# A two-layer encoder trunk on one core: the first attention head's K, Q and V of a chunk projected k tile by k tile together

## The chip, the core and the metric

The kernel runs on one core of a Trainium2 chip. Its engines are TensorE (PE, matrix products), VectorE (DVE), ScalarE (ACT) and GpSimd (POOL); SyncE (SP) issues nearly all DMAs. Each engine works through its own queue in order, and the engines wait for one another by semaphores. The metric is the device time of one launch in microseconds (us). The time before is the median of 3 runs.

## The reference, cut to what matters

The input is x with 1024 tokens of 1024 channels, and a conditioning vector c. Two layers follow one another, each a mixer and an MLP, each of these with an RMSNorm that is shifted and scaled by projections of c. Layer 0 mixes by convolution and gating, layer 1 by differential attention with 8 heads. The change touches the place between the MLP of layer 0 and the attention:

```
x = x + gate * (square(relu(hdn @ mlp_w1[0])) @ mlp_w2[0])
shift, scale, gate = split(c_act @ mix_mod_w[1] + mix_mod_b[1], 3)
hdn = modulate(rmsnorm(x, mix_norm_g[1]), shift, scale)
q, k, v = split(hdn @ w_qkv, 3)          # 8 heads, two maps of 64 channels each
p = softmax(q k^T / 8 + bias)            # both maps
attn = p[0] - lam * p[1]                 # then attn @ v, a norm per head, w_out
```

## The kernel before

**Layout.** Channels lie on the 128 partitions, tokens along the free dimension. A k tile is 128 channels (KT = 8 of them), a chunk is 512 tokens (C = 512, NC = 2 of them). x[m][c] is one 128x512 tile.

**Products.** All projections are in float32 accuracy from a rounded format: a weight w is kept as whi (rounded) and wlo (the rest), an activation as hh and hl. mm3 (L132) adds three matmuls into one PSUM tile: whi with hh (L134), whi with hl (L135), wlo with hh (L136). A 128x512 output of 1024 inputs takes 8 k tiles, so 24 matmuls.

**Weights.** prep (L107) loads 128x1024 numbers into raw, casts them to whi on ACT (L112), and makes wlo in one of two ways: with an engine given, that engine subtracts (L114); without, ACT writes the negative of whi (L116) and a DMA from POOL's queue adds the weights to it from memory (L117). raw, whi and wlo have 3 buffers each. A Stream hands out the weights in order and prepares `ahead` more than the one asked for.

**The norm.** Norm.add squares each x tile on ACT (sq, L229) and sums on DVE (ss, L234 and L237). fin sums over the partitions with a matmul against ones (the statistic, L241, two passes), then v on DVE (L202), ln and r on ACT (L211, L213) and three refining steps on DVE (L215 to L217). h then makes for each of the 8 k tiles ht on DVE (L246), hh on ACT (L253) and hl on DVE (L254).

**The end of the MLP.** mlp works in seven products per group, each of 48 matmuls; in the last group, in this order, X3 completes x of chunk 0, Z and X4 complete x of chunk 1 (updates on L746). to_attn(nrm, c), the norm for the attention, is put off by `soon`: a list of functions with a count, which `tick` lowers and calls when it falls below zero. For chunk 0 it is called in the middle of Z. For chunk 1 it is called in the attention, at the second tick there, that is ahead of chunk 0's Q. to_attn also stores x to memory (xsp) for the last head, between the k tiles of h.

**The first head.** qkv(hd) is a generator that projects K, Q and V of one head in units of one output and one chunk. For head 0 the order of the units is K, Q, V of chunk 0, then K, Q, V of chunk 1 (UNITS); for other heads the generator is run between the parts of the softmax of the head before it, as many k tiles as QUOTA says. A unit takes a PSUM bank (tag mm, 2 buffers), 24 matmuls, and its evictions: K by two casts and two subtractions (L913 to L916), Q likewise and with copies by DMA (L920 to L928), V by a copy, four transposes and a split (L931 to L936). The scores S have 2 buffers of two banks each. Head 0 has nothing to run beside: its generator is emptied before the first softmax. ws, the stream of the heads' weights, prepares one ahead; its low halves are made on DVE for head 0 and the first weight of head 1, on POOL from then on.

**What sets the order.** The program is written once, straight through; a planner then decides the order on each engine's queue. It plays the program through with estimated durations, and whenever an engine comes free it takes, of the instructions whose inputs are ready and whose buffers are free in its play, the one with the best rank. The rank is the place in the program; `tc.high_priority(offset=n)` moves what stands in it n places ahead. On the chip the queues then run in the order so fixed, whatever is late.

Of the kernel before, what the change touches and what calls it, by code (L numbers as in the profile page):

```python
# [10 lines left out]
F32 = mybir.dt.float32  # L11
# [7 lines left out]
P = 128  # L19
D = 1024  # L20
T = 1024
KT = D // P
C = 512
NC = T // C
H = 8
# [22 lines left out]
def trunk(ctx: ExitStack, tc: tile.TileContext, t_in, out):  # L48
    nc = tc.nc
    dve, act, pool, pe, sp = nc.vector, nc.scalar, nc.gpsimd, nc.tensor, nc.sync  # L50

    def f32(ap):
        return ap.bitcast(F32)

    def opened(**kw):
        return tc.tile_pool(reuse_waits="tile", **kw)
# [29 lines left out]
    def load(dst, src):  # L86
        sp.dma_start(out=dst, in_=src)
# [3 lines left out]
    def bank():  # L91
        return psb[-1].tile([P, C], F32, name="ps", tag="mm")
# [7 lines left out]
    def tick(n=1):  # L100
        for e in later:
            e[0] -= n
        while later and later[0][0] < 0:
            later.pop(0)[1]()
# [27 lines left out]
    def mm3(ps, wh, wl, ah, al, first, last, resumed=False):  # L132

        pe.matmul(ps, wh, ah, start=first, stop=False, skip_group_check=resumed)  # L134
        pe.matmul(ps, wh, al, start=False, stop=False, skip_group_check=resumed)  # L135
        newest[0] = pe.matmul(ps, wl, ah, start=False, stop=last, skip_group_check=resumed)  # L136

    def kcol(k):
        return slice(k * P, (k + 1) * P)
# [117 lines left out]
    def split(out_h, out_l, src, lo_eng=None):  # L257
        act.copy(out=out_h, in_=src)  # L258
        (lo_eng or dve).tensor_tensor(out=out_l, in0=src, in1=f32(out_h), op=ALU.subtract)  # L259


    def open_x():
        st = ExitStack()
        xp = st.enter_context(opened(name="xp", bufs=1, side="right"))
        return st, [[xp.tile([P, C], F32, name=f"x{m}_{c}") for c in range(NC)] for m in range(KT)]

    xst, x = open_x()
# [83 lines left out]
    with opened(name="mix", bufs=1) as mp, ExitStack() as pst:  # L351
        first_ps = ExitStack()
        psb.append(first_ps.enter_context(opened(name="gps", bufs=8, space=PSUM)))
        nrm = Norm()
# [3 lines left out]
        h = [[None] * NC for _ in range(KT)]  # L358
# [80 lines left out]
        psum = pst.enter_context(opened(name="mixps", bufs=6, space=PSUM))  # L439
# [5 lines left out]
        for j in range(4):  # L445
            js = slice(j * C, (j + 1) * C)
            ps = bank()
# [34 lines left out]
        for c in range(NC):  # L482
            vps = [bank() for _ in range(4)]
            for j in range(4):
                wh, wl = wv.get(4 * c + j)
# [26 lines left out]
        ps = bank()  # L512
# [48 lines left out]
        xst, x = open_x()  # L561
# [5 lines left out]
        nrm = Norm()  # L567
# [72 lines left out]
        h = [[None] * NC for _ in range(KT)]  # L640
# [229 lines left out]
    xsp = dram.tile([KT, NC, P, C], F32, name="xsp")  # L870

    def to_attn(nrm, c):
        nrm.fin(c)
        for m in range(KT):
            h[m][c] = nrm.h(c, m, x[m][c], 2)
            load(xsp[m, c], x[m][c])

    mlp(0, 1, to_attn)


# [5 lines left out]
    psum = atps.enter_context(opened(name="atps", bufs=2, space=PSUM))  # L886
    psb.append(psum)
    if True:
        ws = Stream([t_in["wqkv"][m] for hd in range(H) for m in (8 + hd, hd, 16 + hd)], ahead=1, eng=dve)
        SC = -(64 ** -0.5)  # L890
        QUOTA = [(2, 3, 0, 0), (2, 2, 2, 1)] * 4
        QUOTA_LAST = [(2, 2, 0, 0), (2, 2, 1, 1)] * 3 + [(0, 2, 0, 0), (0, 4, 0, 0)]
# [2 lines left out]
        def qkv(hd):  # L895
            K = [ap.tile([P, T], F32R, name=f"K{j}", tag="K", bufs=4) for j in range(2)]
            Vh = ap.tile([P, KT, P], F32R, name="Vh", tag="V", bufs=4)
            Vl = ap.tile([P, KT, P], F32R, name="Vl", tag="V", bufs=4)
            Q = [None] * NC
            res = (K, Q, Vh, Vl)  # L900
            yield res
            for which, c in UNITS[hd > 0]:
                cs = slice(c * C, (c + 1) * C)
                wh, wl = ws.get(3 * hd + which)
                tick()
                ps = bank()
                for k in range(KT):
                    mm3(ps, wh[:, kcol(k)], wl[:, kcol(k)], h[k][c][0], h[k][c][1], k == 0, k == KT - 1)
                    if k < KT - 1:
                        yield None  # L910
                with tc.high_priority(offset=300):
                    if which == 0:
                        act.copy(out=K[0][0:64, cs], in_=ps[0:64])  # L913
                        act.copy(out=K[1][64:128, cs], in_=ps[64:128])
                        dve.tensor_tensor(out=K[0][64:128, cs], in0=ps[0:64], in1=f32(K[0][0:64, cs]), op=ALU.subtract)
                        dve.tensor_tensor(out=K[1][0:64, cs], in0=ps[64:128], in1=f32(K[1][64:128, cs]), op=ALU.subtract)  # L916
                    elif which == 1:
                        qs = [ap.tile([P, C], F32R, name="Q", tag="Q", bufs=10) for _ in range(4)]
                        Q[c] = qs
                        act.activation(out=qs[0][0:64], in_=ps[0:64], func=AF.Copy, scale=SC)  # L920
                        act.activation(out=qs[2][64:128], in_=ps[64:128], func=AF.Copy, scale=SC)
                        dve.scalar_tensor_tensor(out=qs[1][0:64], in0=ps[0:64], scalar=SC, in1=f32(qs[0][0:64]),
                                                 op0=ALU.mult, op1=ALU.subtract)
                        dve.scalar_tensor_tensor(out=qs[3][64:128], in0=ps[64:128], scalar=SC, in1=f32(qs[2][64:128]),
                                                 op0=ALU.mult, op1=ALU.subtract)
                        for q in (0, 1):
                            load(f32(qs[q][64:128]), f32(qs[q][0:64]))
                            load(f32(qs[2 + q][0:64]), f32(qs[2 + q][64:128]))  # L928
                    else:
                        vT = tmp.tile([P, C], F32, name="vT", tag="ss", bufs=2)  # L930
                        act.copy(out=vT, in_=ps)  # L931
                        pt = bank()
                        for n in range(4):
                            pe.transpose(pt[:, n * P:(n + 1) * P], vT[:, n * P:(n + 1) * P], ident)
                        vs = slice(c * 4, c * 4 + 4)
                        split(Vh[:, vs, :].rearrange("p a b -> p (a b)"), Vl[:, vs, :].rearrange("p a b -> p (a b)"), pt)  # L936
                yield None
# [125 lines left out]

        wo = Stream([t_in["wo1"][m] for m in range(KT)], ahead=0, eng=pool)
        gen = qkv(0)
        cur = next(gen)
        for _ in gen:
            pass
        ws.eng = pool
        tick(9)  # L1070
        xst.close()
        condp.close()
# [42 lines left out]
    xst, x = open_x()  # L1115
# [3 lines left out]
    with opened(name="wops", bufs=8, space=PSUM) as psum:  # L1119
# [8 lines left out]
        h = project(wo.get, o, ks8, 2, 3, part=(mid, (w7h, w7l)))  # L1128
# [88 lines left out]
```

## Time and profile before

| | |
|---|---|
| median of 3 runs | 2280.48 us (2279.56 to 2282.11) |
| the profiled execution | 2281.83 us |
| its span, first to last instruction | 2279.8 us |
| PE busy | 2193.8 us (96%) |
| DVE busy | 1819.4 us (80%) |
| ACT busy | 1214.2 us (53%) |
| POOL busy | 222.3 us (10%) |
| mean granted clock of PE | 0.989 |

Times in the trace are counted from the first instruction. A row of the timeline has the start, the time from the first start to the last end of the instructions merged in it, the engine, the line, the operation, output and inputs, the count, and in brackets how long the engine stood idle before it and what ended that. Matmuls are pipelined and their ends are modelled, so consecutive rows overlap, and the distance between starts is what a matmul costs. The granted clock is the share of full speed that PE was given.

### The profile page before, as it was taken

What the parts mean: (1) busy time and instruction counts of PE and PEld (TensorE: products, weight loads), DVE (VectorE), ACT (ScalarE), POOL (GpSimd) and SP (SyncE); (2) the same over time, 40 slices, a digit from 0 to 9 for tenths busy, and PEclk for the clock granted to TensorE, in tenths of its full rate; (3) what the DMA queues carried; (4) which work ended last, traced back from release to release, by engine and by line L of the source; (5) the groups of instructions that cost most, each with busy time, mean ns of one, the idle gap of its engine ahead of it and who ended that gap; (6) DMA issues with size and microseconds to landing.
All of it is one profiled execution on the core that took longest, in us unless ns stands there. A gap on an engine that the chain in (4) does not pass through costs nothing. (4 is left out here: it accounts for less than half of the span.)

```text
span 2279.8 us, 27567 instructions
## 1 busy us (share of the span) xinstructions
PE 2193.8 (96%) x10144; PEld 1803.2 (79%) x10144; DVE 1819.4 (80%) x2555; ACT 1214.2 (53%) x1790; POOL 222.3 (10%) x138
## 2 busy tenths in 40 slices
PE   4999898999999999989999999999999999999997
PEld 3778676878888888868888888877778888888886
DVE  7899879995976967978887887885799659577597
ACT  5677646633535435446566666653475354353455
POOL 0485000000000000001111110110000000000003
PEclk9999999999999999989999999999999999999999
DMA  9474774658267275343444433452362561633702
GB/s 352 123 158 108 242 229 174 260 181 292 100 218 271 89 254 193 103 151 55 90 105 84 110 74 69 107 166 82 123 231 86 168 212 56 226 125 122 246 39 74
DMA packets 118038, 350.37 MB, mean 154 GB/s; under 512 B 21040, under 2 KB 23984, under 8 KB 116880
## 3 DMA queue, kind: packets, MB, share of 16 engines
q1 hardware_dynamic: 113728, 333.41, 45.0%
q0 software_dynamic: 4176, 15.21, 3.8%
q8 instruction: 80, 1.31, 0.2%
q14 instruction: 54, 0.44, 0.1%
HBM read 294.99 MB, written 53.58 MB: 153 GB/s over the span
## 5 line engine op out<-in xcount | busy, mean ns | idle before, releaser
L135 PE MATMUL ps<-b,whi 128*128 128x512 f32 (+1 forms) x1808 | 701.4, 389 | 5.9 <-DVE b L259 5.9
L134 PE MATMUL ps<-b,whi 128*128 128x512 f32 (+1 forms) x1808 | 692.3, 389 | 6.3 <-ACT b L258 4.9
L136 PE MATMUL ps<-b,wlo 128*128 128x512 f32 (+1 forms) x1808 | 695.0, 389 | 1.6 <-DVE wlo L259 1.6
L258 ACT CAST whi<-raw 128x1024 fp32r<-128x1024 f32 (+1 forms) x225 | 236.5, 1051 | 355.9 <-PE ps L135 318.5
L135 PEld LDWEIGHTS ps<-b,whi 128*128 128x128 f32 x1808 | 340.7, 188 | 80.0 <-DVE b L259 9.7
L134 PEld LDWEIGHTS ps<-b,whi 128*128 128x128 f32 x1808 | 341.1, 189 | 78.7 <-ACT b L258 6.2
L136 PEld LDWEIGHTS ps<-b,wlo 128*128 128x128 f32 x1808 | 341.1, 189 | 72.1 <-DVE wlo L259 2.0
L259 DVE TENSOR_TENSOR wlo<-raw,whi 128x1024 fp32r<-128x1024 f32 (+1 forms) x225 | 274.8, 1221 | 139.5 <-ACT whi L258 137.2
L134 PE MATMUL ps<-hh,whi 128*128 128x512 f32 x576 | 230.8, 403 | 15.0 <-ACT hh L253 12.5
L135 PE MATMUL ps<-hl,whi 128*128 128x512 f32 x576 | 228.9, 399 | 5.6 <-DVE hl L254 5.5
L136 PE MATMUL ps<-hh,wlo 128*128 128x512 f32 x576 | 227.7, 399 | 3.2 <-DMA wlo<-in_wa 3.2
L965 ACT ACTIVATE L<-L,mn 128x1024 f32<-128x1024 f32 x128 | 147.1, 1150 | 90.8 <-DVE mn L963 89.4
L746 DVE SCALAR_TENSOR_TENSOR x<-ps,mod,x 128x512 f32<-128x512 f32 x220 | 160.7, 751 | 41.3 <-PE ps L136 40.7
L963 DVE CUSTOM_DVE_ANT_0 L<-S,B 128x1024 f32<-128x1024 f32 x128 | 156.0, 1223 | 34.8 <-PE pt L985 17.5
L114 POOL TENSOR_TENSOR wlo<-raw,whi 128x1024 fp32r<-128x1024 f32 x24 | 64.3, 2680 | 1058.0 <-PE S L960 684.6
L258 ACT CAST b<-f 128x512 fp32r<-128x512 f32 x192 | 118.1, 619 | 76.8 <-PE ps L136 75.1
L134 PEld LDWEIGHTS ps<-hh,whi 128*128 128x128 f32 x576 | 110.5, 192 | 41.4 <-ACT hh L253 15.5
L259 DVE TENSOR_TENSOR b<-f,b 128x512 fp32r<-128x512 f32 x192 | 129.7, 690 | 10.3 <-ACT b L258 10.3
L135 PEld LDWEIGHTS ps<-hl,whi 128*128 128x128 f32 x576 | 110.4, 192 | 30.5 <-DVE hl L254 8.7
L136 PEld LDWEIGHTS ps<-hh,wlo 128*128 128x128 f32 x576 | 110.7, 192 | 28.6 <-DMA wlo<-in_wa 3.6
L151 DVE CUSTOM_DVE_ANT_0 mraw<-mraw,cact 128x1024 f32<-128x1024 f32 x96 | 116.6, 1222 | 12.6 <-DMA mraw<-in_modw 12.6
L735 ACT COPY f<-ps 128x512 f32<-128x512 f32 x96 | 56.0, 588 | 123.5 <-PE ps L136 123.3
(201 smaller groups left out, 3469.8 us busy)
## 6 DMA issues: line engine op xcount, KB each, us to landing
b<-tspl SPq DMA_DIRECT2D x168, 512.0 KB, 5.2
raw<-in_wm SPq DMA_DIRECT2D x128, 512.0 KB, 4.8
mraw<-in_modw SPq DMA_DIRECT2D x96, 512.0 KB, 4.6
tspl<-b SPq DMA_DIRECT2D x56, 512.0 KB, 5.3
raw<-in_wqkv SPq DMA_DIRECT2D x24, 512.0 KB, 7.2
raw<-in_wo SPq DMA_DIRECT2D x17, 512.0 KB, 5.0
x<-in_xT SPq DMA_DIRECT2D x32, 256.0 KB, 5.5
tsr<-tsp SPq DMA_DIRECT2D x8, 1024.0 KB, 10.0
```

The source lines that it names most:

```text
L114: eng.tensor_tensor(out=lo, in0=raw, in1=f32(hi), op=ALU.subtract)
L134: pe.matmul(ps, wh, ah, start=first, stop=False, skip_group_check=resumed)
L135: pe.matmul(ps, wh, al, start=False, stop=False, skip_group_check=resumed)
L136: newest[0] = pe.matmul(ps, wl, ah, start=False, stop=last, skip_group_check=resumed)
L151: i = dve.tensor_tensor_reduce(out=raw, in0=raw, in1=cact, op0=ALU.mult, op1=ALU.add, scale=1.0, scalar=0.0, accum_out=acc)
L258: act.copy(out=out_h, in_=src)
L259: (lo_eng or dve).tensor_tensor(out=out_l, in0=src, in1=f32(out_h), op=ALU.subtract)
L735: act.copy(out={"X1": c11, "Y1": c22, "X2": c12}[p], in_=ps)
L746: dve.scalar_tensor_tensor(out=x[m][c], in0=ps, scalar=gate(d, m), in1=x[m][c], op0=ALU.mult, op1=ALU.add)
L963: dve.tensor_tensor_reduce(out=L, in0=S, in1=win, op0=ALU.add, op1=ALU.min, scale=1.0, scalar=3e38, accum_out=mn)
L965: act.activation(out=L, in_=L, func=AF.Exp, bias=mn, scale=-1.0, accum_out=s[:, j:j + 1])
```

## The change

- to_attn makes the norm and all eight pairs hh, hl first and stores x afterwards; for chunk 0 norm and pairs are ranked 200 places ahead.
- For head 0, K, Q and V of a chunk are projected together: three PSUM tiles (the two halves of an S buffer and a bank), and per k tile the three products one after the other. The evictions follow for K, Q and V as before.
- The norm of chunk 1 is called (tick(9)) after the products of chunk 0 and before those of chunk 1.
- The three weights of head 0 are prepared with adding DMAs (no engine given), none ahead; after the products of chunk 1 the stream goes over to one ahead and POOL, so the first weight of head 1 too is made on POOL and asked for only then.

```diff
     def to_attn(nrm, c):
-        nrm.fin(c)
+        with tc.high_priority(offset=0 if c else 200):
+            nrm.fin(c)
+            for m in range(KT):
+                h[m][c] = nrm.h(c, m, x[m][c], 2)
         for m in range(KT):
-            h[m][c] = nrm.h(c, m, x[m][c], 2)
             load(xsp[m, c], x[m][c])
...
-        ws = Stream([t_in["wqkv"][m] for hd in range(H) for m in (8 + hd, hd, 16 + hd)], ahead=1, eng=dve)
+        ws = Stream([t_in["wqkv"][m] for hd in range(H) for m in (8 + hd, hd, 16 + hd)], ahead=0)
...
+            together = []
             for which, c in UNITS[hd > 0]:
                 cs = slice(c * C, (c + 1) * C)
-                wh, wl = ws.get(3 * hd + which)
-                tick()
-                ps = bank()
-                for k in range(KT):
-                    mm3(ps, wh[:, kcol(k)], wl[:, kcol(k)], h[k][c][0], h[k][c][1], k == 0, k == KT - 1)
-                    if k < KT - 1:
-                        yield None
+                if hd == 0:
+
+                    if which == 0:
+                        if c == 1:
+                            tick(9)
+                        w3 = [ws.get(i) for i in range(3)]
+                        S = psum.tile([P, T], F32, name="S", tag="S", bufs=2)
+                        together = [S[:, :C], S[:, C:], bank()]
+                        for k in range(KT):
+                            for i in range(3):
+                                mm3(together[i], w3[i][0][:, kcol(k)], w3[i][1][:, kcol(k)], h[k][c][0], h[k][c][1],
+                                    k == 0, k == KT - 1)
+                        if c == 1:
+                            ws.ahead, ws.eng = 1, pool
+                    ps = together[which]
+                else:
...
-        ws.eng = pool
         tick(9)
         xst.close()
```

More of the change, by code (lines that the diff above doesn't have):

```diff
@@ L901, in qkv @@
             yield res
+            together = []
             for which, c in UNITS[hd > 0]:
                 cs = slice(c * C, (c + 1) * C)
-                wh, wl = ws.get(3 * hd + which)
-                tick()
-                ps = bank()
-                for k in range(KT):
-                    mm3(ps, wh[:, kcol(k)], wl[:, kcol(k)], h[k][c][0], h[k][c][1], k == 0, k == KT - 1)
-                    if k < KT - 1:
-                        yield None
+                if hd == 0:
[13 more added lines that the diff above has]
+                else:
+                    wh, wl = ws.get(3 * hd + which)
+                    tick()
+                    ps = bank()
+                    for k in range(KT):
+                        mm3(ps, wh[:, kcol(k)], wl[:, kcol(k)], h[k][c][0], h[k][c][1], k == 0, k == KT - 1)
+                        if k < KT - 1:
+                            yield None
                 with tc.high_priority(offset=300):
```

## The prediction

> **What bounds the kernel now.** I read the page's busy times first, then the stretches around the place of the change, then who made TensorE (PE) wait there, then that stretch engine by engine in order of time.
>
> ```profile
> PE 2193.8 (96%) x10144; PEld 1803.2 (79%) x10144; DVE 1819.4 (80%) x2555; ACT 1214.2 (53%) x1790; POOL 222.3 (10%) x138
> ```
>
> ```profile
> 940.00:974.50 34.50, 34.49 (x150) 27.71 (x148) 31.39 (x47) 16.49 (x24) 0.00 (x0) 1.00 0.42 143
> 974.50:1027.60 53.10, 44.45 (x166) 33.32 (x166) 40.12 (x61) 27.35 (x42) 3.37 (x2) 0.87 0.41 136
> 1027.60:1080.00 52.40, 52.00 (x273) 43.89 (x272) 42.21 (x73) 31.71 (x51) 4.46 (x3) 1.00 0.27 55
> ```
>
> Columns: stretch, length, then busy time and count for each engine, the granted clock, DMA share. PE is the bound. It is busy for all of the 34.5 us before the stretch from 974.50 and for 52.00 of the 52.40 us after it, at full clock; in between it issues only 166 instructions in 53.10 us, at a mean clock of 0.87. The changed code lies in this stretch: the last MLP product ends at its start, the first head's projections fill it. Both neighbours are limited by PE's own work, so what is won or lost here should reach the end of the program unchanged, and nothing outside it has a gap that the change could close.
>
> What PE waited for in it:
>
> ```profile
> PE ps L135 <- DVE hl L254: 4.2, 3, 2.7
> PE ps L134 <- ACT hh L253: 2.1, 1, 2.1
> PE ps L134 <- ACT ln L211: 2.0, 1, 2.0
> ```
>
> ```profile
> 968.20 1.02 PE L241 MATMUL ps<-ss,ones_r 128*128 128x512 f32 x2
> ...
> 970.45 0.39 PE L134 MATMUL ps<-b,whi 128*128 128x512 f32 x1
> ...
> 973.17 0.39 PE L134 MATMUL ps<-b,whi 128*128 128x512 f32 x1
> ...
> 976.74 0.49 PE L134 MATMUL ps<-hh,whi 128*128 128x512 f32 x1 [2.05 <-ACT hh L253]
> 979.90 0.80 PE L135 MATMUL ps<-hl,whi 128*128 128x512 f32 x1 [2.66 <-DVE hl L254]
> ```
>
> From 970.45 to 973.17 run twelve matmuls: 2.72 / 12 = 0.227 us each. The 166 instructions are 6 x 24 = 144 projection matmuls, 12 of the first scores, 8 short transposes and the two passes of one statistic. 156 x 0.227 = 35.4 us; for the ten others I estimate 1.2 us (the two passes of a statistic end 1.02 us after their start, half of it drain, and a transpose has a quarter of the columns). So 36.6 us of work take 53.1 us: **16.5 us are lost**, 4.2 + 2.1 + 2.0 = 8.3 us as waits, the rest mostly as slow clock. That is the whole sum that can be won, 0.7% of the span.
>
> The slow clock, in consecutive slices of 3.41 us (the same columns):
>
> ```profile
> 985.14:988.55 3.41, 3.41 (x8) 2.55 (x9) 3.41 (x6) 1.53 (x3) 0.00 (x0) 0.50 0.00 0
> 988.55:991.96 3.41, 2.78 (x9) 1.35 (x8) 2.75 (x5) 0.51 (x2) 0.00 (x0) 1.00 0.00 0
> 991.96:995.37 3.41, 1.50 (x7) 1.24 (x8) 2.42 (x5) 2.45 (x4) 0.00 (x0) 1.00 0.01 2
> 995.37:998.78 3.41, 3.41 (x10) 2.63 (x9) 3.34 (x6) 1.25 (x2) 0.00 (x0) 0.51 0.00 0
> ```
>
> At 0.50 the first slice issues 8 matmuls, against 3.41 / 0.227 = 15 at full clock: a slow slice costs 7 x 0.227 = 1.6 us. A slice with PE busy 2.78 us is followed by one at full clock, even though that one is busy only 1.50 us itself; this one is followed by a slow one (0.51). So a hole of about 2 us can cost another 1.6 us.
>
> **The change part by part.** What feeds the first projection, on VectorE (DVE) and ScalarE (ACT):
>
> ```profile
> 965.93 1.22 DVE L114 TENSOR_TENSOR wlo<-raw,whi 128x1024 fp32r<-128x1024 f32 x1
> 967.06 0.69 DVE L237 TENSOR_TENSOR ss<-ss,sq 128x512 f32<-128x512 f32 x1
> ...
> 974.05 0.75 DVE L746 SCALAR_TENSOR_TENSOR x<-ps,mod,x 128x512 f32<-128x512 f32 x1
> 974.72 2.07 DVE L246 SCALAR_TENSOR_TENSOR ht<-x,gA,r 128x512 f32<-128x512 f32 x3
> 976.70 0.75 DVE L746 SCALAR_TENSOR_TENSOR x<-ps,mod,x 128x512 f32<-128x512 f32 x1
> 977.36 1.22 DVE L114 TENSOR_TENSOR wlo<-raw,whi 128x1024 fp32r<-128x1024 f32 x1
> 978.50 0.69 DVE L237 TENSOR_TENSOR ss<-ss,sq 128x512 f32<-128x512 f32 x1
> 979.10 2.07 DVE L254 SCALAR_TENSOR_TENSOR hl<-ht,mod,hh 128x512 fp32r<-128x512 f32 x3
> ```
>
> ```profile
> 968.33 1.03 ACT L112 CAST whi<-raw 128x1024 fp32r<-128x1024 f32 x1
> 970.44 0.69 ACT L211 ACTIVATE ln<-ps,eps 128x512 f32<-128x512 f32 x1 [1.09 <-DVE v L202]
> 971.16 0.63 ACT L213 ACTIVATE r<-ln 128x512 f32<-128x512 f32 x1
> 974.50 1.04 ACT L112 CAST whi<-raw 128x1024 fp32r<-128x1024 f32 x1 [2.70 <-PE ps L135]
> 975.45 0.62 ACT L229 ACTIVATE sq<-x 128x512 f32<-128x512 f32 x1
> 975.99 1.93 ACT L253 ACTIVATE hh<-ht,mod 128x512 fp32r<-128x512 f32 x3
> ```
>
> (a) *Start of the first chunk.* The normalised pairs hh, hl come from a chain: sum of squares (ss), statistic at 968.20, ln, r, ht, hh at 975.99, hl at 979.10. PE is free from 974.50 and gets its second matmul at 979.90. With the low halves made by adding DMAs, DVE loses the 128x1024 subtractions of L114: the one at 965.93 stands ahead of the last ss (967.06 - 965.93 = 1.13 us), the one at 977.36 ahead of hl (978.50 - 977.36 = 1.14 us). The one between the chain's steps near 970 lies beside ln and r on ACT and is worth nothing. The higher rank can drop what else was let in: x at 974.05 (0.67), the cast and the square ahead of hh (975.99 - 975.4 where ht is ready, 0.6), x and ss ahead of hl (977.36 - 976.70, 979.10 - 978.50: 1.26). But the planner fills any slot that it sees free, and rank orders only what is ready together; the rank was already ahead of these in program order. I take half of 2.5. hl then starts at 979.10 - 1.13 - 1.14 - 1.25 = 975.6 and PE's first hl matmul at 976.3. Two hh matmuls fit before: loss 976.3 - 974.5 - 0.45 = 1.4 us; bounds 0.6 (all of the 2.5) and 2.6 (none). Of the old clock loss there, a hole of 1.4 lies between the two cases seen (0.6 and 1.9 us): half of 1.6, 0.8 us, bounds 0 and 3.2.
>
> (b) *Through the first chunk.* Three products together take 9 x 0.227 = 2.04 us per k tile; DVE makes a pair in 2 x 0.66 us (three ht take 976.70 - 974.72 = 1.98), and with six ss of 0.60 among eight pairs in 1.77. So PE is the slower and no longer waits for DVE. But the low halves are late. V's weight slot is freed with the last MLP product (cast at 974.50), Q's at 968.33. From cast to low half:
>
> ```profile
> L116 ACT ACTIVATE wlo<-whi x29: 1037/1057/1065, 17.7 to 333.0; 128x1024 fp32r<-128x1024 f32 x29
> ...
>   PE ps L136: 3.2, 1
> ...
> DMA to landing us min/median/max: 5.3/5.9/9.9
> ```
>
> 1.05 (cast) + 1.06 (negated copy, three more of these on ACT) + 5.9 (median landing of an adding DMA, of 29 before 340 us) = 8.0 us: Q at 976.3, V at 982.5, each up to 1 us later if ACT makes an hh first. GpSimd is idle here (POOL 0.00 in the stretch before), so its queue holds back neither DMA. Until 982.5 PE can run K and Q alone, 1.36 us per pair, about the pace of DVE, and takes up V afterwards: the order loses nothing if the plan foresaw the landing. I take 0.5 us, bounds 0 and 3.2, the one wait that such a DMA caused (3.2 us). By the Trainium skill, "DMA: Bandwidth & Descriptors", Anatomy of one DMA, a DMA from this queue takes an estimated 2.0 + 524288 / 436e3 = 3.2 us; the row's 5.9 is not that, and by the page this term would be 0.
>
> The 72 matmuls are 16.3 us; the first chunk ends at 974.5 + 1.4 + 0.8 + 0.5 + 16.3 = 993.5.
>
> (c) *Between the chunks.* This is new. The second chunk's norm is now called after all of the first chunk's products, so its statistic ranks behind 72 matmuls. Its sums are ready near 988 (first ht near 973, then eight pairs 10.6, six ss 3.6 and an x 0.7 on DVE), but PE then has ready products up to 993.5. From statistic to PE's first use of hh took 976.74 - 968.20 = 8.5 us, of which 0.67 + 0.6 were let in; I take 7.4 us, bounds 7.2 and 8.5. Only the statistic, four transposes and two score matmuls can run meanwhile (1.3 us): 6.1 us idle, bounds 5.9 and 7.2, where the old order had 2.0. A hole that long brings one or two slow slices: 2.5 us, bounds 1.6 and 3.2. The first hl comes some 0.3 us (0.2 to 0.5) later than the three hh matmuls cover: an hl takes 0.75 us, they 0.68, and DVE starts it only when hh is there.
>
> By the Trainium skill, "TensorE: Matmul & The Clock Gate", Part 1, the clock is judged in free-running windows of 3413 ns and falls after an idle one; the slices above have just that length and alternate so, but the one at 995.37 is slow after a hole of only 2.0 us, so here less than an idle window is enough. By the page's rule (only holes above some 3 us count) the 0.8 us of (a) would be 0 and the sum 0.8 us lower.
>
> (d) *Between second chunk and next head.* K, Q and V end together, so the weights of the next head, whose slots they hold, are made at the end, and low halves on GpSimd:
>
> ```profile
> 1019.92 2.40 POOL L114 TENSOR_TENSOR wlo<-raw,whi 128x1024 fp32r<-128x1024 f32 x1 [684.65 <-PE S L960]
> ```
>
> Cast 1.05 + 2.40 after K's last high matmul, nine matmuls (2.0 us) before the end: 1.5 us, and up to 2.3 us more if the four evictions of K and Q go first on ACT. PE has the second half of a score, transposes and two high products to fill with: 1.5 us lost, bounds 0.2 and 2.8; before, V's second chunk covered this (0.3 us lost).
>
> (e) *Nothing else.* The stores of x are issued behind the eight pairs; they are read only in the last head. Accumulating in a score buffer costs nothing, as no score can start before K and Q are out of it.
>
> Sum of the losses after: 1.4 + 0.8 + 0.5 + 6.1 + 2.5 + 0.3 + 1.5 = 13.1 us, against 16.5: **3.4 us won**. The profiled execution took 2281.83 us (span 2279.8 and 2.0 around it), 1.35 above the median of the runs, 2280.48; so 2278.4 in its terms and 2277.1 for the median. All low bounds give 0.6 + 0 + 0 + 5.9 + 1.6 + 0.2 + 0.2 = 8.5 (8.0 won); all high ones 2.6 + 3.2 + 3.2 + 7.2 + 3.2 + 0.5 + 2.8 = 22.7 (6.2 lost).
>
> **The rivals.** *The statistic is taken early.* If PE waits for an hl or a low half when the second sums are ready, the plan puts the statistic in that hole, as it set the one at 968.20 amid products. From 988 the chain ends at 995.4, so the hole is 995.4 - 993.5 = 1.9, not 6.1, and a slow slice less: 3.4 + 4.2 + 1.0 = 8.6 won, 2272. Against it: the backlog of V, which the late low half makes longer.
>
> *The low halves stall PE (slower).* PE takes its queue in order. Where the plan put V's third matmul ahead of K and Q of later tiles, and the DMA lands later than planned, all of PE stands. Price: the slowest landing 9.9 - 5.9 = 4.0 and the wait of 3.2 us seen: 7.2 us, so 2277.1 + 7.2 = 2284. It ends above the time before once the stall passes 3.4 us. For it: V's cast cannot start before 974.50. Against it: 28 of 29 such DMAs made PE wait for nothing, though most were asked for earlier.
>
> *The rank and the pairing change nothing.* If gap fillers stay as they are and the first hole moves from the k tiles to the space between the chunks: terms (a) and (c) at their high ends, 1.2 + 2.4 + 1.1 + 0.7 = 5.4 worse, 2282.5. For it: rank did not keep the cast at 974.50 from standing ahead of hh.
>
> **How the numbers follow.** Likeliest, the trade as summed: 0.45, mostly 2273 to 2282. Early statistic 0.28; low-half stall 0.17; nothing gained 0.10. A measurement of this kernel can tell 0.2%, 4.6 us: faster is below 2275.9, slower above 2285.0. Faster: 0.85 of the early case (0.24), 0.38 of the trade (0.17), together 0.41. Slower: 0.5 of the stall (0.09), 0.2 of the last (0.02), 0.07 of the trade (0.03), together 0.14. Same: 0.45. The range takes in the early case and the stall: 2269 to 2285.
>
> **What would show it.** Right: the first hl matmul by 977; no L114 on DVE before 1010; PE's longest hole between the chunks, ended by an hh of the second chunk, with the statistic directly ahead of it; a slow slice behind it; another hole of 1 to 3 us before the next head, ended by a low half from GpSimd. Wrong: the statistic amid the first chunk's products; a wait of PE for wlo by DMA; PE's first hole still above 4 us; or a time outside the stretch that moves.

## The result: slower by 0.24%, and the profile after

Over 15 runs each the changed kernel took 2284.62 us (2279.83 to 2287.02) and the kernel before 2279.26 us (2273.00 to 2282.34): ratio 1.0024, 95% interval 1.0017 to 1.0031, 5.4 us slower. Predicted were 3.4 us won. The profiled execution of the changed kernel took 2285.2 us, span 2283.4.

Busy times, from the page of the changed kernel:

```profile
PE 2190.3 (96%) x10144; PEld 1801.0 (79%) x10144; DVE 1814.3 (79%) x2551; ACT 1216.8 (53%) x1793; POOL 227.7 (10%) x142
```

The three stretches of the prediction (start:end, length, busy and count of PE, PEld, DVE, ACT, POOL, granted clock, DMA):

```profile
940.00:974.50 34.50, 34.29 (x149) 27.37 (x147) 29.23 (x44) 18.46 (x27) 1.75 (x2) 1.00 0.50 157
974.50:1027.60 53.10, 39.48 (x154) 30.29 (x154) 33.16 (x51) 25.40 (x39) 4.48 (x3) 0.90 0.42 126
1027.60:1080.00 52.40, 50.75 (x263) 41.96 (x264) 43.69 (x76) 31.46 (x52) 6.47 (x3) 1.00 0.26 66
```

In the middle one PE issues 154 instructions instead of 166, and in the third, which held no gap before, it is busy 50.75 us instead of 52.00. What PE waited for in the middle one:

```profile
PE S L134 <- ACT hh L253: 9.3, 2, 6.3
PE S L978 <- DVE K L934: 2.3, 1, 2.3
PE ps L953 <- ACT vT L950: 1.2, 1, 1.2
PE ps L136 <- DMA wlo<-in_wqkv: 0.5, 1, 0.5
PE S L135 <- DVE hl L254: 0.3, 1, 0.3
```

Where these waits lie, in PE's timeline:

```profile
973.92 0.39 PE L136 MATMUL ps<-b,wlo 128*128 128x512 f32 x1
977.30 0.50 PE L134 MATMUL S<-hh,whi 128*128 128x512 f32 x1 [3.00 <-ACT hh L253]
...
978.38 0.80 PE L135 MATMUL S<-hl,whi 128*128 128x512 f32 x1 [0.34 <-DVE hl L254]
...
998.09 0.66 PE L953 MATMUL ps<-ident,vT 128*128 128x128 f32 x4 [1.19 <-ACT vT L950]
998.58 1.02 PE L241 MATMUL ps<-ss,ones_r 128*128 128x512 f32 x2
1005.90 0.80 PE L134 MATMUL S<-hh,whi 128*128 128x512 f32 x1 [6.29 <-ACT hh L253]
...
1024.01 0.39 PE L136 MATMUL ps<-hh,wlo 128*128 128x512 f32 x1
1026.69 0.50 PE L978 MATMUL S<-K,Q 128*128 128x512 f32 x1 [2.29 <-DVE K L934]
...
1028.07 0.48 PE L134 MATMUL ps<-hh,whi 128*128 128x512 f32 x1
```

Chunk 0's last product starts at 996.50, so nothing but a statistic and four transposes runs in the 9.2 us to 1005.90. At the end all three outputs are finished together, and 3.8 us pass before the next head's products.

The third stretch shows in DVE's timeline, in the rows that read the scores of head 0 (L963 before, L982 after). First the kernel before: its first, second and 17th score; then the changed kernel:

```profile
1019.92 1.22 DVE L963 CUSTOM_DVE_ANT_0 L<-S,B 128x1024 f32<-128x1024 f32 x1
1026.18 1.23 DVE L963 CUSTOM_DVE_ANT_0 L<-S,B 128x1024 f32<-128x1024 f32 x1 [3.48 <-PE S L960]
...
1080.20 1.23 DVE L963 CUSTOM_DVE_ANT_0 L<-S,B 128x1024 f32<-128x1024 f32 x1 [0.24 <-PE S L960]
```

```profile
1027.46 1.22 DVE L982 CUSTOM_DVE_ANT_0 L<-S,B 128x1024 f32<-128x1024 f32 x1
1034.03 1.23 DVE L982 CUSTOM_DVE_ANT_0 L<-S,B 128x1024 f32<-128x1024 f32 x1 [2.96 <-PE S L979]
...
1084.95 1.23 DVE L982 CUSTOM_DVE_ANT_0 L<-S,B 128x1024 f32<-128x1024 f32 x1 [0.24 <-PE S L979]
```

The last MLP product starts 0.38 us earlier in this execution than in that of before (973.92 against 974.30), so the scores are read 7.9, 8.2 and 5.1 us later. **PE shift** below is the same comparison for PE: each matmul counts 0.227 us per 512 columns, the start is taken at which PE has done equal work in both traces, and the difference at 940 us is taken off. For the changed kernel it is +2.6 us at 1035 and +5.1 at 1200: 2.6 us are lost in the stretch, 2.5 more in head 0's attention.

What PE waited for in the third stretch, in the kernel before and in the changed one:

```profile
PE S L959 <- DVE mn L963: 0.4, 1, 0.4
```

```profile
PE ps L1015 <- ACT AT L258: 1.1, 1, 1.1
PE S L978 <- DVE mn L982: 0.4, 1, 0.4
PE ps L953 <- ACT vT L950: 0.2, 1, 0.2
```

AT is the transposed result of a softmax, which ACT copies for the product with V. This wait, at 1070.59, is new, and it is at the end of the softmax's chain; what remains of the 2.5 us lies in smaller gaps between matmuls.

### The profile page after: what moved, and what is told of

The parts are those of the page before. It is cut to its first block, busy times and chain, and to the rows that moved or that the text cites. A ratio compares the mean times of both kernels' runs of the same rounds, so it can differ in the third digit from the quotient of the medians.

```text
span 2283.4 us, 27568 instructions
## 1 busy us (share of the span) xinstructions
PE 2190.3 (96%) x10144; PEld 1801.0 (79%) x10144; DVE 1814.3 (79%) x2551; ACT 1216.8 (53%) x1793; POOL 227.7 (10%) x142
## 5 line engine op out<-in xcount | busy, mean ns | idle before, releaser
L134 PE MATMUL ps<-hh,whi 128*128 128x512 f32 x544 | 217.3, 402 | 11.4 <-ACT hh L253 11.0
L136 PE MATMUL ps<-hh,wlo 128*128 128x512 f32 x544 | 214.6, 398 | 2.8 <-DMA wlo<-in_wa 2.3
L135 PE MATMUL ps<-hl,whi 128*128 128x512 f32 x544 | 215.5, 398 | 0.8 <-DVE hl L254 0.7
L982 DVE CUSTOM_DVE_ANT_0 L<-S,B 128x1024 f32<-128x1024 f32 x128 | 155.8, 1222 | 31.0 <-PE pt L1004 16.3
L134 PEld LDWEIGHTS ps<-hh,whi 128*128 128x128 f32 x544 | 103.9, 191 | 35.0 <-ACT hh L253 13.0
L136 PEld LDWEIGHTS ps<-hh,wlo 128*128 128x128 f32 x544 | 104.4, 192 | 27.1 <-DMA wlo<-in_wa 2.7
L135 PEld LDWEIGHTS ps<-hl,whi 128*128 128x128 f32 x544 | 104.4, 192 | 22.9 <-DVE hl L254 1.9
L978 PE MATMUL S<-K,Q 128*128 128x512 f32 x256 | 108.9, 426 | 3.0 <-DVE K L934 2.3
```

Source lines behind the costliest of these rows:

```text
L978: pe.matmul(S[:, sl], self.Q[c][2 * j][:, qs], self.K[j][:, sl], start=True, stop=False)
L982: dve.tensor_tensor_reduce(out=L, in0=S, in1=win, op0=ALU.add, op1=ALU.min, scale=1.0, scalar=3e38, accum_out=mn)
```

## The experiments

Each ratio is to the kernel before, run in the same rounds, 11 or 12 runs of the kernel (six of e2); 0.001 is 2.3 us. "Second score" is its shift against the kernel before, in one profiled execution each, as are the PE shifts.

| kernel | ratio, 95% interval | PE shift at 1035 | second score | PE shift at 1200 |
|---|---|---|---|---|
| changed | 1.0024 (1.0017 to 1.0031) | +2.6 | +8.2 | +5.1 |
| e1 | 1.0022 (1.0013 to 1.0031) | -3.5 | +1.8 | +0.2 |
| e2 | 1.0031 (1.0019 to 1.0042) | +6.1 | +11.7 | +8.6 |
| e3 | 1.0026 (1.0017 to 1.0035) | +5.8 | +11.4 | +8.3 |
| e4 | 1.0014 (1.0005 to 1.0023) | +5.2 | +5.2 | +5.1 |
| e6 | 1.0023 (1.0014 to 1.0032) | +0.7 | +5.4 | +3.1 |
| e8 | 1.0006 (0.9998 to 1.0015) | -3.9 | +1.5 | -0.2 |
| e9 | 1.0002 (0.9993 to 1.0011) | -5.6 | +0.3 | -2.8 |
| e10 | 1.0007 (0.9997 to 1.0016) | -1.8 | +3.4 | +0.7 |
| e11 | 0.9977 (0.9968 to 0.9986) | -5.8 | -5.4 | -4.4 |
| e12 | 1.0024 (1.0016 to 1.0033) | +0.8 | 0.0 | +6.1 |
| e14 | 0.9994 (0.9982 to 1.0005) | -2.1 | -1.7 | -0.7 |
| e15 | 1.0010 (1.0000 to 1.0021) | +0.4 | +0.8 | +1.7 |

**e1, the norm of chunk 1 ahead of chunk 0's products**

```diff
-                        if c == 1:
+                        if c == 0:
                             tick(9)
```

> The changed kernel with one thing undone: the norm of chunk 1 is called ahead of chunk 0's products instead of behind them. The changed kernel stands 5.4 us above the one before (2284.6 against 2279.3).
> Theory A (late statistic: the 9.2 us between chunk 0's last matmul at 996.50 and the next real product at 1005.90 are what the change lost): the sums of chunk 1 are ready at about 989.2 (last ss at 988.61), so the statistic comes near 989 to 990 amid chunk 0's products, and with the 7.3 us from statistic to hh that the changed kernel shows, the first hh of chunk 1 is there at about 996.5, where chunk 0 ends. The hole shrinks from 9.2 to 1 to 2.5 us and one slow slice (1.6 us) goes: 7 to 9 us less in the stretch, 2276 to 2278, 1 to 3 us under the kernel before.
> Rival (the second loss is elsewhere: K, Q and V of chunk 1 end together, so the first softmax begins late and PE waits in head 0's attention at 1062 to 1074 for some 2.5 us whenever chunk 1 ends): the 2.5 us stay or grow, as PE gets to head 1's products earlier too: 2278 to 2280, level with the kernel before.
> Rival (DVE's order: squares and sums of chunk 1 now compete with the pairs of chunk 0 and DVE is the slower one there): PE waits for hl during chunk 0 for as long as is saved behind it: 2282 to 2285.

2284.96 us: at first sight nothing. The trace says otherwise. The statistic runs at 990.83 amid chunk 0's products, PE is 3.5 us ahead of the kernel before at 1035, level with it from 1070 to 1580, and then loses over 7 us in one place:

```profile
1589.17 1.13 PE L1028 MATMUL ps<-sq,ones_r 128*128 128x512 f32 x2 [1.12 <-ACT sq L1026]
1594.80 0.80 PE L134 MATMUL ps<-th,whi 128*128 128x512 f32 x1 [4.50 <-DVE v L1032]
```

The output projection's product waits for the PSUM bank of the head's norm statistic. In the changed kernel this product has the other bank, and no such wait. e8 tests this.

**e8, the same with the other bank**

```diff
-                        if c == 1:
-                            tick(9)
                         w3 = [ws.get(i) for i in range(3)]
                         S = psum.tile([P, T], F32, name="S", tag="S", bufs=2)
                         together = [S[:, :C], S[:, C:], bank()]
+                        if c == 0:
+                            tick(9)
```

> As in e1, chunk 1's norm is called ahead of chunk 0's products, but behind the line that takes the three PSUM tiles. Every engine's order of instructions is that of e1; only which of the two banks each product gets is different, and with it one wait 570 us later: in e1 the output projection's product at 1594.80 has to wait 4.5 us for the bank of the last head's norm statistic (and runs a slow slice behind it).
> Theory (the bank): that hole goes, 5 to 7.5 us less than e1 (2285.0).
> Theory D (what counts at the end of head 0's attention is the later of two things, PE's own progress and the start of the first softmax): in e1 PE is 3.5 us ahead of the kernel before at 1028, but the first score is read at 1019.7 (1020.1 in the kernel before's terms), where the kernel before reads it at 1019.92, and by 1070 the lead is gone. So this kernel is level with the kernel before: 2278 to 2280.
> Rival (PE's lead is carried, its loss at 1050 to 1070 was chance of that one execution): 2275 to 2276.5.
> Rival (the bank makes no difference, the 7.3 us at 1590 were chance): 2284 to 2286.

2279.31 us, ratio 1.0006: under e1 by 3.6 us by the ratios, 5.7 by the medians, 7.5 in that place by the traces, though every engine executes the same instructions in the same order. The product behind the statistic starts at 1592.67, 0.56 us after it, without a wait. So the late norm costs 1.0024 - 1.0006 = 0.0018 of the time, 4 us, but calling it early only brings the kernel level: as theory D has it, PE's lead of 3.9 us at 1035 is gone at 1200.

**e2, low halves on DVE; e3, no higher rank**

```diff
-...ahead=0)
+...ahead=0, eng=dve)
```

> The changed kernel with one thing undone: the low halves of the first head's three weights are made by subtraction on DVE again (still none prepared ahead), not by a negated copy on ACT and an adding DMA.
> Theory B (the adding DMAs cost at the start): the negated copy of V's weight at 975.60 (1.04 us on ACT) no longer stands ahead of the first hh at 976.55, which then starts about 0.95 us earlier, and the wait of 0.52 us for V's low half by DMA goes; but DVE gets three subtractions of 1.22 us, and the one for V (cast ending near 975.1) stands ahead of hl or between the pairs. If the copies cost more than the subtractions: 1 to 1.5 us less than the changed kernel, 2283.
> Rival (they were worth having): the first hl comes 1.1 to 1.2 us later, and chunk 0 as a whole 1 to 3 us: 2285.5 to 2288.
> Theory A (late statistic) by itself says nothing of this run: the hole between the chunks stays at 8 to 9.5 us and the kernel within 1.5 us of the changed one.

2285.77 us, 1.2 us over the changed kernel and within the intervals. The first hh does come 0.95 us earlier after the MLP (wait 2.05 us for 3.00), the first hl 1.1 us later than there (wait 2.42 for 0.34): the adding DMAs trade one for the other and are worth about nothing.

```diff
-        with tc.high_priority(offset=0 if c else 200):
+        with tc.high_priority(offset=0):
```

> The changed kernel without the higher rank of chunk 0's norm (the order inside the norm, pairs first and stores after, stays).
> Theory (rank changed nothing: x and ss, made where DVE was free, still stand ahead of ht and hl in the changed kernel): within 1 us of the changed kernel, the same rows at 973 to 979.
> Rival (rank is what brought the first hl from 979.10 to 977.58): the first hl 0.7 to 1.4 us later, 2285.5 to 2286.

2285.11 us. The order of all instructions on all engines is the same as with the rank: it changed nothing. This is a second measurement of the changed kernel (1.0026 beside 1.0024), and it shows what one execution is worth: its PE shift at 1035 is +5.8 instead of +2.6, at a mean clock of 0.87 in the stretch instead of 0.90. Sizes below 3 us are therefore read from the ratios.

**e4, chunk 1 unit by unit; e6, V of chunk 1 apart; both with the late norm**

```diff
-                if hd == 0:
+                if hd == 0 and c == 0:
...
-                    tick()
+                    tick(9 if hd == 0 and which == 0 else 1)
```

> The changed kernel with K, Q and V together for chunk 0 alone; chunk 1 is projected unit by unit (K, Q, V) as before, the norm of chunk 1 still called behind chunk 0's products.
> Theory C (three outputs of chunk 1 that end together cost the 2.3 us wait for K at 1026.69, and the late start of the first softmax costs some 2.5 us in head 0's attention at 1062 to 1074): with K and Q of chunk 1 done 16 and 11 matmuls of products earlier, both losses go: 3 to 5 us less than the changed kernel, 2279.6 to 2281.6. The hole between the chunks is not touched (8 to 10 us).
> Rival (unit by unit, chunk 1's K has to wait for each hl of DVE, 3 matmuls of 0.227 us per pair that takes DVE 1.32 us): K's 8 k tiles take 8 x 1.32 = 10.6 us instead of 5.4, so 5 us are lost there and the gain is used up or more: 2284 to 2288.

2282.33 us. As theory C said, nothing more is lost after 1035 (+5.2 there, +5.1 at 1200), but the stretch itself is worse: behind the hole PE starts chunk 1 alone on K's pairs, at a granted clock of 0.57 over ten microseconds, and the wait for K stays (2.2 us). Theory and rival each have half.

```profile
1003.64:1013.64 10.00, 9.17 (x23) 6.13 (x23) 9.93 (x16) 4.88 (x7) 0.00 (x0) 0.57 0.74 261
```

```diff
-                if hd == 0:
+                if hd == 0 and (which, c) != (2, 1):
...
-                        w3 = [ws.get(i) for i in range(3)]
+                        w3 = [ws.get(i) for i in range(3 - c)]
...
-                        together = [S[:, :C], S[:, C:], bank()]
+                        together = [S[:, :C], S[:, C:]] + ([] if c else [bank()])
...
-                            for i in range(3):
+                            for i in range(3 - c):
```

> The changed kernel, its late norm kept, but in chunk 1 only K and Q together and V alone behind them.
> Theory D: the hole of 9 us between the chunks stays, PE's own progress stays 0.5 to 2.6 us behind the kernel before (the 2.3 us wait for K near 1026.7 may go), but the first score is read 4 to 5 us earlier than in the changed kernel (near 1022.5 to 1023.5), so the second loss of 2.5 us at 1062 to 1074 goes: 2279.5 to 2281.7, 3 to 5 us under the changed kernel.
> Rival (the late norm is all of the loss): no more than 1 us under the changed kernel, 2283.6 to 2284.6.

2283.31 us, 1.3 us under the changed kernel. The rival is nearer; why, e9 shows.

**e9, norm early (as e8) and V of chunk 1 apart (as e6)**

> As e8, and in chunk 1 only K and Q are projected together; V follows alone (24 matmuls, 5.4 us), so that it covers the evictions of K and Q and the start of the softmax, as V did in the kernel before.
> Theory D: the first score is read 4 to 5.4 us earlier than in e8 (near 1015 to 1016), PE's lead of 3.5 us is no longer lost in head 0's attention: 2275 to 2276.5, 2.5 to 4 us under the kernel before.
> Rival (DVE sets the pace: K and Q together take 1.36 us per k tile and DVE makes a pair in 1.32, but it also has the splits of chunk 0's K, Q and V to do, so PE waits for pairs and the lead is gone by 1025): 2278 to 2280.
> Rival (the first softmax was not the cause of the loss): as e8.

2278.40 us, not told apart from e8. V did not go behind: the order took its products wherever one of K or Q was planned to wait, so that K and Q were still among the last. ACT's timeline shows the end of it: two casts for the next head's weights, then K's evictions, 7 us after the last pair was made.

```profile
1004.36 0.72 ACT L253 ACTIVATE hh<-ht,mod 128x512 fp32r<-128x512 f32 x1 [0.60 <-DVE ht L246]
1011.19 2.00 ACT L112 CAST whi<-raw 128x1024 fp32r<-128x1024 f32 x2 [6.11 <-PE S L135]
1013.10 0.57 ACT L932 CAST K<-S 64x512 fp32r<-64x512 f32 x1
```

The shift of -2.8 at 1200 does not last either: between 1500 and 1510, in the kernel before's time, it goes to +0.1. There two DVE instructions stand beside GpSimd (rs takes 2.37 us for 0.22, L 2.28 for 1.28), and PE waits 1.6 us for a score to be read. That this happens in the other executions too is not shown.

**e10, as e9, low halves on GpSimd**

```diff
-...ahead=0)
+...ahead=0, eng=pool)
```

> As e9, and the low halves of the first head's three weights are subtracted on GpSimd instead of made by a negated copy on ACT and an adding DMA.
> Theory B (the copies and the late landing cost at the start): the copy of 1.04 us ahead of the first hh at 976.55 goes, hh and hl come 0.9 us earlier and the wait of 0.5 us for V's low half too: 1 to 1.5 us less than e9.
> Rival (DVE and GpSimd disturb each other: DVE's ht, hl and sums take longer beside a GpSimd subtraction): level with e9 or up to 2 us more; DVE's 0.66 us rows near 976 would be longer.

2279.14 us, no gain. hh comes 0.95 us earlier after the MLP, as theory B said, and hl later: the wait for it is 3.79 us. DVE's and GpSimd's timelines:

```profile
965.07 3.18 DVE L237 TENSOR_TENSOR ss<-ss,sq 128x512 f32<-128x512 f32 x2
...
975.11 4.17 DVE L246 SCALAR_TENSOR_TENSOR ht<-x,gA,r 128x512 f32<-128x512 f32 x3
...
964.51 2.39 POOL L114 TENSOR_TENSOR wlo<-raw,whi 128x1024 fp32r<-128x1024 f32 x1 [627.83 <-DVE ss L237]
...
975.84 2.88 POOL L114 TENSOR_TENSOR wlo<-raw,whi 128x1024 fp32r<-128x1024 f32 x1 [3.50 <-ACT whi L112]
```

Three ht take 2.07 us elsewhere and 4.17 here, one ss 0.68 and here up to 2.38: the long one of each starts beside a GpSimd instruction and ends within 0.6 us of its end (966.90 and 978.72). The rival holds.

**e11, as e9, with V held behind K and Q**

```diff
+                    behind = newest[0]
                     for k in range(KT):
-                        mm3(ps, ...)
+                        first = pe.matmul(ps, wh[:, kcol(k)], h[k][c][0], start=k == 0, stop=False)
+                        if hd == 0 and k == 0:
+                            tc.add_manual_dep(first.ins, behind.ins.name, NOSYNC, reason="V behind K and Q")
...
```

> As e9, but V of chunk 1 is held behind the last product of K and Q by a dependency on PE (no semaphore). In e9 the order put V's products between those of K and Q wherever a pair was late in the plan, so the three ended together after all and the first score was read only 0.7 us earlier than in e8 (1015.8, which is 1019.7 in the kernel before's terms; the kernel before: 1019.92).
> Theory D (the end of head 0's attention follows the later of PE's progress and the softmax chain that begins with the first score): K and Q are out some 5 us earlier, the first score is read near 1017 in the kernel before's terms and the second right behind it (1026.2 there), so PE's lead of 4 to 5 us at 1028 is kept to 1080: 2273.5 to 2275.5, some 4 us under the kernel before.
> Rival (the lead was lost for another reason, say the next head's weights, which come out of GpSimd at 2.4 us each): level with e9, 2277.5 to 2279.
> Rival (K and Q alone run at DVE's pace, 1.33 us a pair against 1.36 us of products, and every late pair is now a hole that V no longer fills): 2278 to 2280.

2273.81 us, ratio 0.9977 (0.9968 to 0.9986): 5 us faster than the kernel before, and the fastest of all. The first score is not read as early as I had expected, but the second follows it at once (columns as above; 4.1 us to be added for the kernel before's terms), and no wait of PE is listed between 1050 and 1075:

```profile
1015.40 1.23 DVE L987 CUSTOM_DVE_ANT_0 L<-S,B 128x1024 f32<-128x1024 f32 x1
1016.69 1.22 DVE L987 CUSTOM_DVE_ANT_0 L<-S,B 128x1024 f32<-128x1024 f32 x1
```

Against e9, which differs in the dependency alone, PE is level at 1035 (-5.8 and -5.6) and 3.6 us ahead at 1080 (-6.4 and -2.8): this much is won in head 0's attention. The rest of the 5.7 us between them by the ratios lies behind it.

The same 53.1 us from the end of the MLP hold 192 PE instructions here, against 184 in e8 and 155 in the changed kernel (one row of each):

```profile
970.39:1023.49 53.10, 47.42 (x192) 36.58 (x192) 41.37 (x65) 30.25 (x46) 8.04 (x4) 0.94 0.56 167
```

```profile
975.75:1028.85 53.10, 45.90 (x184) 35.43 (x184) 36.87 (x57) 28.51 (x43) 7.90 (x4) 0.94 0.55 164
```

```profile
974.12:1027.22 53.10, 39.46 (x155) 30.29 (x154) 33.27 (x51) 25.40 (x38) 4.10 (x3) 0.90 0.43 127
```

**e12, the kernel before with a late first softmax**

```diff
-                    dve.tensor_tensor_reduce(out=L, in0=S, in1=win, ...)
+                    for _ in range(11 if self.hd + qb + j == 0 else 1):
+                        dve.tensor_tensor_reduce(out=L, in0=S, in1=win, ...)
```

> The kernel before, with one DVE instruction on the first score of head 0 done eleven times instead of once (the same result each time; 10 x 1.23 = 12.3 us more on DVE, which stood idle for most of 1021 to 1032). PE's work and weights are untouched; only the first softmax is later: its second score is read at about 1033 to 1034 instead of 1026.2, as late as in the changed kernel (1034.4).
> Theory D: PE runs head 1's products ahead and then waits in head 0's attention, as in the changed kernel: 4 to 7 us more than the kernel before (the changed kernel lost 5.1 us by 1080 with its scores 7 to 8 us late), 2282.5 to 2285.5.
> Rival (PE's own progress alone counts, a late softmax is made up for out of slack): 0 to 1.5 us more, 2278.5 to 2280.

2283.83 us, ratio 1.0024: as much as the whole change costs, with PE's projections untouched. The rival falls. But the delay is not where it was expected: the order put the read of the second score among the repeats, at 1022.41, as early as before (3.7 us to be added for the kernel before's terms). What is late is the last read of the first score (1034.43), and with it the first step that joins both maps, by 12.3 us (kernel before, then e12):

```profile
1029.18 1.28 DVE L973 SCALAR_TENSOR_TENSOR L<-L,rs 128x1024 f32<-128x1024 f32 x1
```

```profile
1037.76 1.29 DVE L974 SCALAR_TENSOR_TENSOR L<-L,rs 128x1024 f32<-128x1024 f32 x1
```

The shift is +0.8 at 1035, +2.5 at 1080 and +6.1 at 1200: theory D's time is met, but only 1.7 us are lost up to 1080. Another 2.0 and 1.6 go where a DVE instruction stands beside a GpSimd subtraction (osb 2.79 us for 0.75 at 1087.57, L 3.32 for 1.28 at 1158.47). So the run shows what a late softmax costs, not by which waits, and it does not tell the delay from the 12.3 us of work added to DVE, which had 4.6 us free from 1021 to 1032 and was not idle for most of it.

**e14, the kernel before with chunk 1 as in e11; e15, e11 with the late norm**

```diff
+                if hd == 0 and c == 1 and which < 2:
+                    if which == 0:
+                        w2 = [ws.get(i) for i in range(2)]
+                        tick()
...
+                            for i in range(2):
+                                mm3(together[i], ...)
+                    ps = together[which]
+                else:
...
```

> The kernel before (chunk 0 unit by unit, its weights with low halves on DVE, norm of chunk 1 where it was) with chunk 1 alone changed: K and Q together and V held behind them, as in e11.
> Theory (e11 wins by two things: chunk 0 together keeps PE busy while its pairs are made, which puts PE 5 to 6 us ahead at 1000, and chunk 1's order keeps that): without the first, PE is level with the kernel before at 1010 and only the second score is read earlier (right behind the first instead of 6.3 us later): 2277.5 to 2279.5.
> Rival (all of e11's gain lies in chunk 1's order and the early softmax): 2273.5 to 2275.5.

2278.32 us, ratio 0.9994, level with the kernel before and 3.9 us (0.0017) over e11. So the change's main idea, chunk 0 together, is worth something, if chunk 1 doesn't give it back. (e14 also keeps the weights and the norms of the kernel before, so the 3.9 us are the price of all that e11 changes outside chunk 1's order.)

```diff
-                        if c == 0:
-                            tick(9)
...
+                        if c == 1:
+                            tick(9)
```

> As e11, but with the changed kernel's late norm of chunk 1 (called behind chunk 0's products).
> Theory A and D together: the hole of some 9 us between the chunks is back, PE is level with the kernel before at 1010; K and Q of chunk 1 are out some 5 us earlier than in the changed kernel and V covers the start of the softmax, so the changed kernel's wait of 2.3 us at 1026.7 and its second loss at 1062 to 1074 are both gone: 2279.5 to 2281.5, 5 to 7 us above e11 (the price of the late norm alone) and 3 to 5 under the changed kernel (the price of the late softmax).
> Rival (the late norm by itself is harmless once the softmax starts early): 2274 to 2276.

2281.88 us, ratio 1.0010: 7.5 us (0.0033) over e11, which is the late norm's price alone, and 3.2 us (0.0014) under the changed kernel.

## Why the prediction was wrong

By the PE shift at 1200 the forecast was 8.5 us off, 3.4 won against 5.1 lost. Some 6 of these are terms of the sum for the stretch that were too small, above all (a) and (b); they alone turn the gain into a loss. The other 2.5 are a term that was put at nothing, (e). The sizes are those of one execution: e3, the same program, lost 5.8 us in the stretch and also 2.5 behind it.

**(e) Nothing else: the step that failed by its mechanism.** "Both neighbours are limited by PE's own work, so what is won or lost here should reach the end of the program unchanged." PE was busy 52.00 of 52.40 us behind the stretch, but with head 1's products, run ahead of head 0's softmax; when these are used up, PE has the pace of the softmax. Where the three outputs of chunk 1 end nearly together, the second score comes 4.7 to 5.9 us further behind PE than in the kernel before (the difference of the two columns). These kernels (the changed one, e1, e2, e3, e6, e8, e9) all have the wait of 1.1 us for AT and lose 2.4 to 3.7 us from 1035 to 1200, however far ahead PE is; e10 alone has such a late second score without this wait. Where the second score follows the first at once (e11, e14, e15), and in e4, the wait is missing. So a lead of PE is lost without earlier scores (e8), a late first softmax costs 5.5 us with PE's products untouched (e12, with what is said there), and PE ahead with early scores wins (e11). A busy engine had work in stock; that is not the same as being the bound.

e10, e11, e12, e14 and e15 lose another 2.0 to 2.2 us from 1090 to 1100 (in the kernel before's time) for a different reason. In these five, and in no other, the DVE instruction osb starts 0.46 us behind a GpSimd subtraction and takes 2.8 us; the next read of a score is late, and PE waits 1.7 us for it. First e11, then the kernel before, where osb is through when the subtraction starts:

```profile
1077.89 2.68 POOL L114 TENSOR_TENSOR wlo<-raw,whi 128x1024 fp32r<-128x1024 f32 x1 [6.64 <-ACT whi L112]
1078.35 2.77 DVE L1039 SCALAR_TENSOR_TENSOR osb<-osb,subg,r 128x512 f32<-128x512 f32 x1
1084.20 0.50 PE L983 MATMUL S<-K,Q 128*128 128x512 f32 x1 [1.70 <-DVE mn L987]
```

```profile
1087.18 0.75 DVE L1015 SCALAR_TENSOR_TENSOR osb<-osb,subg,r 128x512 f32<-128x512 f32 x1
1088.40 3.26 POOL L114 TENSOR_TENSOR wlo<-raw,whi 128x1024 fp32r<-128x1024 f32 x1 [6.64 <-ACT whi L112]
```

**(a) and (b), the start and chunk 0.** Predicted 1.4 + 0.8 + 0.5 = 2.7 us lost; from the MLP's end at 974.15 to chunk 0's at 996.73 are 22.6 us for 16.3 us of products, so 6.3 were: 3.8 as waits (3.0 for hh, 0.3 for hl, 0.5 for wlo), most of the rest in a slice at a granted clock of 0.50 from 978.30 to 981.71. I counted the negated copies only on the way to the low halves, not in ACT's own queue; the one for V stands right ahead of hh:

```profile
974.12 1.04 ACT L112 CAST whi<-raw 128x1024 fp32r<-128x1024 f32 x1 [2.73 <-PE ps L135]
975.07 0.62 ACT L229 ACTIVATE sq<-x 128x512 f32<-128x512 f32 x1
975.60 1.04 ACT L116 ACTIVATE wlo<-whi 128x1024 fp32r<-128x1024 f32 x1
976.55 1.32 ACT L253 ACTIVATE hh<-ht,mod 128x512 fp32r<-128x512 f32 x2
```

On DVE x and ss still stand ahead of hl, which starts at 977.58 and not at 975.6; the "half of 2.5" credited to the rank was zero (e3). Nor did the 1.13 us count that were credited to the subtraction ahead of the last ss: the statistic starts at 967.81, as before when the 0.38 us are taken off (968.20), in its place among PE's products. Of the three savings that put hl at 975.6 only the second, 1.14 us, came.

```profile
976.32 0.75 DVE L746 SCALAR_TENSOR_TENSOR x<-ps,mod,x 128x512 f32<-128x512 f32 x1
976.98 0.68 DVE L237 TENSOR_TENSOR ss<-ss,sq 128x512 f32<-128x512 f32 x1
977.58 1.41 DVE L254 SCALAR_TENSOR_TENSOR hl<-ht,mod,hh 128x512 fp32r<-128x512 f32 x2
...
988.61 0.68 DVE L237 TENSOR_TENSOR ss<-ss,sq 128x512 f32<-128x512 f32 x1
```

V's low half by DMA cost 0.5 us, as put down.

**(c) The hole between the chunks: right in kind and place, too small.** The sums were ready near 989 (last row above), the statistic came behind all 72 products, and from statistic to hh took 1005.90 - 998.58 = 7.3 us (predicted 7.4). But it did not start with chunk 0's end: V's copy and its transposes went first, 1.9 us. Idle were 8.3 us (9.2 less 0.9 for statistic and transposes) instead of 6.1. The slow clock and the late hl behind it cost less than the 2.5 and 0.3 put down, 1.5 us (18.3 us for chunk 1's 72 products and two scores, 16.8 at full clock).

**(d) The tail.** Predicted 1.5 us, bounds 0.2 to 2.8; 2.9 were lost (3.8 less 0.9 for two scores and transposes). On ACT two casts for the next head stand ahead (1022.85 to 1024.75), then come K's two casts and, from 1025.95, its subtractions on DVE; GpSimd's low halves, which I had named, end nothing: PE waits for K (2.3 us), so the cause put down for this term was wrong too.

Summed so, 6.3 + 8.3 + 1.5 + 2.9 = 19.0 us against 13.1 predicted and 16.5 before: 2.5 us lost in the stretch (2.6 by the PE shift), and with the 2.5 of (e) 5.1.

**The rivals.** The early statistic did not happen by itself; made so (e8), it is level, not at 2272. The low-half stall gave almost the measured time, 2284, by a cause that isn't there (0.5 us); that 2284.62 lies in the range at all is luck, as the range's upper end stood for that stall. "The rank and the pairing change nothing" was right on the rank.

## What to carry to other kernels

An engine that shows no gap behind a place may be living on work run ahead: before a gain there is carried to the end, find the chain that runs beside it (here scores and softmax) and ask when its first link moves. Products that finish together also deliver together; what a slow chain waits for should be finished first, and what covers it (here V) be held behind by a dependency, since a greedy order will pull it forward. A comparison should also check, far from the change, that no wait has appeared where buffers were merely dealt out differently.

## What the runs showed that I had not expected

- Which of two PSUM banks a product gets cost 3.6 to 5.7 us (e1 against e8), 600 us after the edit.
- While GpSimd subtracts two operands from SBUF, a DVE instruction with two such operands stands still to its end: ss 2.38 us for 0.68 (e10), osb 2.77 for 0.75 (e11). Whether the two meet is a matter of half a microsecond, and it costs PE some 2 us or nothing. By the Trainium skill, "SBUF — State Buffer", section "SBUF: two separate sides", the two engines share one pair of ports, locked for a whole instruction against a DVE operation with two SBUF inputs; these rows agree.
- After e1's wait of 4.5 us PE's matmuls start 0.43 us apart instead of 0.23 from 1595.4 to 1600.5, longer than one slice of 3.41 us.
